# A hybrid encoder step: a third of the modulation's TensorE part goes to the vector engine, the rest is issued in bursts of four column groups

## The chip, the cores and the metric

The kernel runs on one core of a Trainium2 chip, as one program. The metric is the device time of one execution in microseconds (us); lower is better. The core has five engines that run side by side from queues of their own: PE (TensorE, matrix products), DVE (VectorE), ACT (ScalarE), POOL (GpSimd) and SP, which here only starts transfers from memory. Weight loads into the PE array are shown as an engine of their own, PEld.

## The reference, cut to what matters

One layer of a streaming encoder is computed for 256 prompt rows and 32 sample rows of width 2048. A vector `c` per sequence (two sequences, so two vectors) gives six modulation vectors of 2048 values:

```python
cs = jax.nn.silu(c)
mod = cs @ w_mod[l] + b_mod[l]                      # w_mod: 2048 x 12288, float32
sh1, sc1, g1, sh2, sc2, g2 = split(mod, 6)
h = rms_norm(x, norm1_g[l]) * (1 + sc1) + sh1
y, ... = mixer_block(h, ...)                        # w_in, three branches A, B, C, w_branch, w_out
x = x + g1 * y
h = rms_norm(x, norm2_g[l]) * (1 + sc2) + sh2
x = x + g2 * sq_relu_mlp(h, w_up[l], w_down[l])
y = rms_norm(x, final_g)
```

Part 0 and part 1 of the modulation (`sh1`, `sc1`) are needed before the first product, part 2 (`g1`, "the gate of the output projection") only when the output projection has been computed, and parts 3 to 5 later still.

## The kernel before, in words

All big products are float32 products made of three TensorE products each (high half times low half, high times high, low times high), on tiles of 128 x 128 weights against 288 or 290 columns. Weights arrive as 512 KB loads (`raw`, a ring of six buffers, started by SP in program order); ACT makes the high half `whi` (L425), DVE the low half `wlo` (L426), and PE takes both (L412 to L414 in the first stage, L443 to L445 after it). Every load of `w_mod` goes into the same ring of six.

The modulation has a batch of two, so its products are cheap to compute and dear to feed. It is a Python generator, `mods`, advanced one step (one load of 512 KB) at a time between the products. `mod_steps` makes a step; the rates `MODR`, `RS`, `RA`, `RB` ... say how many steps go with one piece of product work (1.5 in the first stage until parts 0 and 1 are through, then 0.2, and 0.4 from the first mixer of branch A).

- **The boot, parts 0 and 1** (`mod_stream`, L277): 8 units of 256 columns and 4 of 512. A load carries 4 row blocks of a 256 column unit or 2 of a 512 column unit. For each row block `k` the array's column group `k % 4` (32 of 128 columns, of which two are used) multiplies `cT` with the load; four groups work side by side and each sums its own quarter of the 16 row blocks. After a unit ACT copies the sums (L282), and `mod_flush` adds the four quarters with a product with `selm` (L348) and the bias on DVE (L349). A 256 column unit has 4 steps, a 512 column unit 8.
- **Part 2, the gate** (`mod_parts`, L329): two halves of 1024 columns, 16 loads each. Each load is one row block of 1024 columns, and four products of 256 columns, one in each column group, take it. After a half one copy and two transposes finish it.
- **Parts 4, 3 and 5** (`mod_part_ve`): four units of 512 columns, 8 loads of two row blocks each. DVE multiplies a load by the two scalars of each row block and adds, four instructions per load (L303 for the first two of a unit, L305 for all others), into two sums `macc`. At the end of a unit eight small products with `ones2` (L75 and L78), a copy and one transpose sum over the partitions.

A step is one load in each of the three forms, and each part has 32 steps, so the count of steps is the same in all. `together` (L72) issues the first of a list of instructions at ordinary priority and the rest right behind it. The order of the instructions on each engine is planned when the program is built, by a list scheduler with simulated times; `high_priority` moves the loads ahead.

One record of the trace is not one product: each float32 product of the modulation leaves two matmul records.

Of the kernel before, what the change touches and what calls it, by code (L numbers as in the profile page):

```python
# [10 lines left out]
F32 = mybir.dt.float32  # L11
# [3 lines left out]
ALU = mybir.AluOpType  # L15
PSUM = bass.MemoryType.PSUM

P = 128
D = 2048
NB = D // P  # L20
# [20 lines left out]
def tile_step(ctx, tc, io, outs):  # L41
    nc = tc.nc
    V, S, G, TE = nc.vector, nc.scalar, nc.gpsimd, nc.tensor

    const = ctx.enter_context(tc.tile_pool(name="const", bufs=1))
    wpool = ctx.enter_context(tc.tile_pool(name="wpool", bufs=3))
    hpool = ctx.enter_context(tc.tile_pool(name="hpool", bufs=3 * NB))
    pmain = ctx.enter_context(tc.tile_pool(name="pmain", bufs=4, space=PSUM))
    paux = ctx.enter_context(tc.tile_pool(name="paux", bufs=2, space=PSUM))

    PRIO = 2500

    MOD_PARTS = (2, 4, 3, 5)
    MOD_VE = (4, 3, 5)


    MODR, RS, RA, RB, RD, RW, RC = 1.5, 0.2, 0.4, 0.3, 0.5, 0.5, 0.25
# [2 lines left out]
    MTAG = ("raw", RAW)  # L60
# [8 lines left out]
    def nm(s):  # L69
        uid[0] += 1  # L70
        return f"{s}_{uid[0]}"

    def together(works):

        first = works[0]()  # L75
        with tc.issue_after(first.ins), tc.high_priority(offset=PRIO):
            for work in works[1:]:
                work()  # L78

    def aux():  # L80
        return paux.tile([P, 512], F32, tag="aux", name=nm("aux"))
# [28 lines left out]
    ident = const.tile([P, P], F32, name="ident")  # L110
# [62 lines left out]
    cT = const.tile([P, NB, 32], F32, name="cT")  # L173
    V.memset(cT, 0.0)
    with tc.high_priority(offset=2 * PRIO):
        ps = aux()
        TE.transpose(ps[:, 0:32], crow, ident[0:32, 0:32])
        S.activation(out=cT[:, :, 0:2].rearrange("p k s -> p s k"),
                     in_=ps[:, 0:32].rearrange("p (s k) -> p s k", s=2), func=AF.Silu)


    ones2 = const.tile([P, 2, 32], F32, name="ones2")
# [72 lines left out]
    def par(name, j, n=1):  # L255
        i, r = off[name]
        return pcols[i][:, r + j:r + j + n]
# [4 lines left out]
    mod = const.tile([P, 6 * NB, 2], F32, name="mod")  # L262
    wm = io["w_mod"][0].rearrange("(k p) n -> p k n", p=P)

    def mod_stream(units):

        for u, (c0, w) in enumerate(units):
            ps = paux.tile([P, 512], F32, tag="modps", name=nm("modps"), bufs=2)
            nk = 1024 // w
            for q in range(NB // nk):  # L270
                with tc.high_priority(offset=PRIO):
                    raw = wpool.tile([P, nk, w], F32, tag="raw", name=nm("raw"), bufs=RAW)
                    nc.sync.dma_start(out=raw, in_=wm[:, nk * q:nk * (q + 1), c0:c0 + w])
                for i in range(nk):
                    k = nk * q + i
                    cg = k % 4
                    TE.matmul(ps[32 * cg:32 * cg + 32, 0:w], cT[:, k, :], raw[:, i, :],  # L277
                              start=k < 4, stop=k >= 12)
                if q == NB // nk - 1:
                    with tc.high_priority(offset=PRIO):  # L280
                        sb = wpool.tile([P, 512], F32, tag="modsb", name=nm("modsb"), bufs=1)
                        S.copy(out=sb[:, 0:w], in_=ps[:, 0:w])  # L282
                    mod_tail.append((c0 // P, w // P, ps, sb))
                if q == 1:
                    mod_flush()
                yield
        mod_flush()

    def mod_part_ve(part):


        for u in range(4):
            c0 = part * D + u * 512
            acc = [wpool.tile([P, 512], F32, tag="macc", name=nm("macc"), bufs=2) for _ in range(2)]
            for q in range(8):
                with tc.high_priority(offset=PRIO):
                    raw = wpool.tile([P, 2, 512], F32, tag=MTAG[0], name=nm("mraw"), bufs=MTAG[1])
                    nc.sync.dma_start(out=raw, in_=wm[:, 2 * q:2 * q + 2, c0:c0 + 512])
                for i in range(2):
                    for s in range(2):  # L300
                        cs = cT[:, 2 * q + i, s:s + 1]
                        if q == 0 and i == 0:
                            V.tensor_scalar_mul(out=acc[s], in0=raw[:, i], scalar1=cs)  # L303
                        else:
                            V.scalar_tensor_tensor(out=acc[s], in0=raw[:, i], scalar=cs, in1=acc[s],  # L305
                                                   op0=ALU.mult, op1=ALU.add)
                if q == 1:
                    mod_flush()
                yield
            ps = paux.tile([P, 512], F32, tag="modps", name=nm("modps"), bufs=2)  # L310
            mod_tail.append((part * NB + u * 4, 0, ps, acc))
        mod_flush()

    def mod_parts(parts):


        for part in parts:
            if part in MOD_VE:
                yield from mod_part_ve(part)
                continue  # L320
            for half in range(2):
                ps = paux.tile([P, 512], F32, tag="modps", name=nm("modps"), bufs=2)
                c0 = part * D + half * 1024
                for k in range(NB):
                    with tc.high_priority(offset=PRIO):
                        raw = wpool.tile([P, 1024], F32, tag=MTAG[0], name=nm("mraw"), bufs=MTAG[1])
                        nc.sync.dma_start(out=raw, in_=wm[:, k, c0:c0 + 1024])
                    for cg in range(4):
                        TE.matmul(ps[32 * cg:32 * cg + 32, 0:256], cT[:, k, :], raw[:, cg * 256:(cg + 1) * 256],  # L329
                                  start=k == 0, stop=k == NB - 1)  # L330
                    if k == 1:
                        mod_flush()
                    yield
                with tc.high_priority(offset=PRIO):
                    sb = wpool.tile([P, 256], F32, tag="modsb", name=nm("modsb"), bufs=1)
                    S.copy(out=sb, in_=ps[:, 0:256])
                mod_tail.append((part * NB + half * 8, 0, ps, sb))
        mod_flush()

    mod_tail = []  # L340

    def mod_flush():

        while mod_tail:
            j, n, ps, sb = mod_tail.pop()
            if n:
                for b in range(n):
                    TE.matmul(ps[:, 2 * b:2 * b + 2], sb[:, b * P:(b + 1) * P], selm, start=True, stop=True)  # L348
                V.tensor_tensor(out=mod[:, j:j + n, :],  # L349
                                in0=ps[:, 0:2 * n].rearrange("p (b s) -> p b s", s=2),  # L350
                                in1=par("b_mod", j, n).unsqueeze(2).to_broadcast([P, n, 2]), op=ALU.add)
            else:
                nb = 2
                if type(sb) is list:
                    nb = 1
                    acc, sb = sb, wpool.tile([P, 256], F32, tag="modsb", name=nm("modsb"), bufs=1)
                    together([partial(TE.matmul, ps[32 * cg:32 * cg + 32, 0:P], ones2[:, s],
                                      acc[s][:, cg * P:(cg + 1) * P], start=s == 0, stop=s == 1)
                              for s in range(2) for cg in range(4)])
                    S.copy(out=sb[:, 0:P], in_=ps[:, 0:P])  # L360
                for b in range(nb):
                    TE.transpose(ps[:, b * P:(b + 1) * P], sb[:, b * P:(b + 1) * P], ident)
                v = ps[:, 0:nb * P].rearrange("p (b g r) -> p g b r", b=nb, r=32)
                m = mod[:, j:j + 4 * nb, :].rearrange("p (g b) s -> p g b s", b=nb)
                V.tensor_tensor(out=m, in0=v[:, :, :, 0:2], op=ALU.add,
                                in1=par("b_mod", j, 4 * nb).rearrange("p (g b) -> p g b", b=nb).unsqueeze(3)
                                .to_broadcast([P, 4, nb, 2]))


    KG = ((0, 2), (2, 2), (4, 2), (6, 2), (8, 4), (12, 4))  # L370
    boot = [(part * D + k0 * P, nk * P) for k0, nk in KG for part in (0, 1)]
    mods = chain(mod_stream(boot), mod_parts(MOD_PARTS))

    mod_count = [0]

# [82 lines left out]
    with tc.high_priority(offset=PRIO):  # L458
        for i in range(8):
            for c, src in ((c, xrow.get((c, i))) for c in range(3)):  # L460
                if src is not None:
                    n, w = src.shape
# [6 lines left out]
    ps = aux()  # L469
    for c, (t0, n) in enumerate(CH):  # L470
        TE.matmul(ps[:, t0:t0 + n], st[:, c, 8:9].to_broadcast([P, P]), ident if c < 2 else sel4,
                  start=True, stop=True)
# [569 lines left out]
    def finish_c(j, vt):  # L1042
        g = j // 2
        pm = aux()
        for c, (t0, n) in enumerate(CH):
# [11 lines left out]
    part = ([(COL_V, j, each(evac_v)) for j in range(0, 8, 2)] + [(COL_U, j, each(evac_u)) for j in range(0, 8, 2)]  # L1057
            + [(COL_XBC, j, each(evac_xbc)) for j in range(8, CVB, 2)]
            + [(COL_GATE + 2 * D, j, each(evac_gate0)) for j in range(0, G0, 2)])
# [7 lines left out]
    for g, (k0, nk) in enumerate(KG):  # L1067
# [7 lines left out]
        m = 4 // nk  # L1075
# [45 lines left out]
    ps = aux()  # L1121
# [36 lines left out]
    ps = transpose_xs()  # L1158
# [103 lines left out]
    parts = [0, NB - 2, NB - 1]  # L1262
# [10 lines left out]
    for q in range(4):  # L1273
        for c, (t0, n) in enumerate(CH):
            w = 2 * P if q == 3 else 4 * P
# [42 lines left out]
```

## Time and profile before

| | before |
|---|---|
| three timed runs | 2085.69, 2086.59, 2087.05 us; median 2086.59 |
| the profiled execution's own time | 2083.99 us |
| its span, first to last instruction | 2082.3 us (1.69 us lie around it) |
| granted TensorE clock, mean | 0.993 |
| PE, PEld, DVE, ACT, POOL busy | 98%, 93%, 70%, 48%, 7% of the span |
| read from memory | 405.05 MB, 197 GB/s over the span |

The profile is of one execution. Start times are counted from its first instruction. Matmuls are pipelined: the start of the next one, not the length of one, says what it took from the array. A busy time is a union of the instructions' spans, so overlaps are counted once.

### The profile page before, as it was taken

The numbers are of one execution on the slowest core, as the hardware profiler recorded it, in microseconds if no ns is written. First come the engines' busy times: TensorE is split into PE (matmuls) and PEld (weight loads), VectorE is DVE, ScalarE is ACT, GpSimd is POOL, SyncE is SP. The second block draws the span as 40 slices with busy tenths as digits, with TensorE's granted clock in tenths as the row PEclk, the third lists the DMA queues.
The fourth block names the chain that finished last, engine by engine and source line by source line (L and its number), as shares of the span: only waits on it lengthen the run. The fifth ranks groups of instructions, "written<-read, shape, count | busy, mean of one in ns | idle before, by whom it ended". The sixth has DMA issues, their size and how long they took to land.

```text
span 2082.3 us, 40240 instructions
## 1 busy us (share of the span) xinstructions
PE 2034.7 (98%) x16248; PEld 1941.9 (93%) x16248; DVE 1453.9 (70%) x2515; ACT 998.1 (48%) x1553; POOL 155.7 (7%) x284
## 2 busy tenths in 40 slices
PE   5999999999999999999999999999999999999997
PEld 3777898989999999999999999999999999999997
DVE  2566566776679987888889998665864455555564
ACT  3423475566555555645534455433443344334443
POOL 3020113011001110010100110000000000000010
PEclk8999999999999999999999999999999999999999
DMA  9888755455666665667777777666665555555552
GB/s 265 258 279 252 232 152 165 147 177 174 203 205 202 204 190 177 212 201 236 239 245 241 219 242 225 196 216 194 213 192 163 168 166 163 165 168 164 163 161 88
DMA packets 364874, 412.29 MB, mean 198 GB/s; under 512 B 14808, under 2 KB 325488, under 8 KB 364688
## 3 DMA queue, kind: packets, MB, share of 16 engines
q1 hardware_dynamic: 360784, 403.97, 62.6%
q0 software_dynamic: 3040, 4.58, 1.0%
q8 instruction: 127, 2.08, 0.4%
q10 hardware_dynamic: 864, 1.18, 0.2%
q14 instruction: 59, 0.48, 0.1%
HBM read 405.05 MB, written 4.62 MB: 197 GB/s over the span
## 4 chain that ended last, share of the span: by engine, by line
PE 60%; ACT 0%; DVE 0%; issue 0%; ACTq 0%
PE mm L445 20%; PE mm L443 20%; PE mm L444 20%; PE aux L1208 0%; PE aux L208 0%; ACT stage L1282 0%; PE aux L879 0%; PE modps L75 0%; PE modps L78 0%; PE aux L78 0%; PE aux L918 0%; PE aux L867 0%; PE aux L75 0%; PE aux L900 0%; PE pr L1265 0%; DVE x L1246 0%
## 5 line engine op out<-in xcount | busy, mean ns | idle before, releaser
L425 ACT CAST whi<-raw 128x1024 fp32r<-128x1024 f32 x568 | 595.2, 1048 | 862.3 <-PE mm L444 646.5
L426 DVE TENSOR_TENSOR wlo<-raw,whi 128x1024 fp32r<-128x1024 f32 x568 | 695.1, 1225 | 411.4 <-ACT whi L425 409.9
L443 PE MATMUL mm<-hlo,whi 128*128 128x288 f32 x1408 | 420.3, 299 | 0.0
L444 PE MATMUL mm<-hhi,whi 128*128 128x288 f32 x1408 | 417.0, 297 | 0.0
L445 PE MATMUL mm<-hhi,wlo 128*128 128x288 f32 x1408 | 414.0, 299 | 0.1
L444 PE MATMUL mm<-h2hi,whi 128*128 128x290 f32 x1024 | 303.5, 297 | 0.0
L445 PE MATMUL mm<-uhi,wlo 128*128 128x288 f32 x1024 | 303.2, 296 | 0.0
L443 PE MATMUL mm<-h2lo,whi 128*128 128x290 f32 x1024 | 303.0, 296 | 0.0
L445 PE MATMUL mm<-h2hi,wlo 128*128 128x290 f32 x1024 | 301.8, 297 | 0.0
L444 PE MATMUL mm<-uhi,whi 128*128 128x288 f32 x1024 | 301.3, 294 | 0.0
L443 PE MATMUL mm<-ulo,whi 128*128 128x288 f32 x1024 | 301.0, 294 | 0.0
L305 DVE SCALAR_TENSOR_TENSOR macc<-mraw,cT,macc 128x512 f32<-128x512 f32 x360 | 262.1, 755 | 26.1 <-DMA mraw<-in_w_mod_dram 25.7
L443 PEld LDWEIGHTS mm<-hlo,whi 128*128 128x128 f32 x1408 | 265.6, 189 | 9.1 <-issue 7.2
L444 PEld LDWEIGHTS mm<-hhi,whi 128*128 128x128 f32 x1408 | 266.0, 189 | 0.4
L445 PEld LDWEIGHTS mm<-hhi,wlo 128*128 128x128 f32 x1408 | 263.7, 189 | 1.7 <-DVE z L614 0.4
L443 PEld LDWEIGHTS mm<-h2lo,whi 128*128 128x128 f32 x1024 | 194.1, 190 | 0.5 <-DVE wlo L426 0.2
L445 PEld LDWEIGHTS mm<-h2hi,wlo 128*128 128x128 f32 x1024 | 193.6, 190 | 0.3 <-issue 0.2
L444 PEld LDWEIGHTS mm<-h2hi,whi 128*128 128x128 f32 x1024 | 193.8, 189 | 0.0
L443 PEld LDWEIGHTS mm<-ulo,whi 128*128 128x128 f32 x1024 | 193.0, 188 | 0.4 <-issue 0.4
L444 PEld LDWEIGHTS mm<-uhi,whi 128*128 128x128 f32 x1024 | 192.4, 188 | 0.0
L445 PEld LDWEIGHTS mm<-uhi,wlo 128*128 128x128 f32 x1024 | 192.2, 188 | 0.1
L412 PE MATMUL mm<-hlo,whi 128*128 128x288 f32 x448 | 139.1, 311 | 0.0
(420 smaller groups left out, 3068.9 us busy)
## 6 DMA issues: line engine op xcount, KB each, us to landing
raw<-in_w_in_dram SPq DMA_DIRECT2D x204, 512.0 KB, 4.3
mraw<-in_w_mod_dram SPq DMA_DIRECT2D x128, 512.0 KB, 4.1
raw<-in_w_up_dram SPq DMA_DIRECT2D x128, 512.0 KB, 3.7
raw<-in_w_down_dram SPq DMA_DIRECT2D x128, 512.0 KB, 3.5
raw<-in_w_mod_dram SPq DMA_DIRECT2D x64, 512.0 KB, 5.0
raw<-in_w_branch_dram SPq DMA_DIRECT2D x48, 512.0 KB, 4.3
raw<-in_w_out_dram SPq DMA_DIRECT2D x32, 512.0 KB, 4.6
raw<-in_w_in_dram SPq DMA_DIRECT2D x56, 256.0 KB, 5.0
```

The costliest lines, as they stand in the source:

```text
L305: V.scalar_tensor_tensor(out=acc[s], in0=raw[:, i], scalar=cs, in1=acc[s], op0=ALU.mult, op1=ALU.add)
L412: TE.matmul(pt, whi[:, i, cs], alo[k], start=i == 0, stop=False)
L425: S.copy(out=whi, in_=raw)
L426: V.tensor_sub(out=wlo, in0=raw, in1=whi)
L443: TE.matmul(pts[b], whi[:, i, cs], alo[k], start=k == 0, stop=False)
L444: TE.matmul(pts[b], whi[:, i, cs], ahi[k], start=False, stop=False)
L445: TE.matmul(pts[b], wlo[:, i, cs], ahi[k], start=False, stop=k == nk - 1)
```

## The change

Three things change, all in the modulation.

1. `mod_stream` collects the row blocks of two loads and issues them after every second load (`mod_cols`): eight products over four column groups for a 256 column unit, four products for a 512 column unit. They go through `together`, last row block first, so that the first one waits for the later load and the others follow it without other work between them.
2. Part 2 goes through `mod_part_ve` like the later parts; `mod_parts` and its branch in `mod_flush` are gone. Order and count of the steps stay: boot, then parts 2, 4, 3, 5, with 32 steps each.
3. The staging tile `modsb` of the tail is declared 128 wide in the room of 512.

```diff
-    MOD_VE = (4, 3, 5)
...
             nk = 1024 // w
+            held = []
             for q in range(NB // nk):
...
-                for i in range(nk):
-                    k = nk * q + i
-                    cg = k % 4
-                    TE.matmul(ps[32 * cg:32 * cg + 32, 0:w], cT[:, k, :], raw[:, i, :],
-                              start=k < 4, stop=k >= 12)
+                held += [(nk * q + i, raw[:, i, :]) for i in range(nk)]
+                if q % 2:
+                    mod_cols(ps, held, w)
+                    held = []
...
+    def mod_cols(ps, held, w):
+        works, begun = [], set()
+        for k, r in reversed(held):
+            cg = k % 4
+            works.append(partial(TE.matmul, ps[32 * cg:32 * cg + 32, 0:w], cT[:, k, :], r,
+                                 start=held[0][0] == 0 and cg not in begun, stop=k == held[0][0] + cg and held[-1][0] == NB - 1))
+            begun.add(cg)
+        together(works)
...
-    def mod_parts(parts):
-        for part in parts:
-            if part in MOD_VE:
-                yield from mod_part_ve(part)
-                continue
-            for half in range(2):
-                ps = paux.tile([P, 512], F32, tag="modps", name=nm("modps"), bufs=2)
-                c0 = part * D + half * 1024
-                for k in range(NB):
...
-                        raw = wpool.tile([P, 1024], F32, tag=MTAG[0], name=nm("mraw"), bufs=MTAG[1])
-                        nc.sync.dma_start(out=raw, in_=wm[:, k, c0:c0 + 1024])
-                    for cg in range(4):
-                        TE.matmul(ps[32 * cg:32 * cg + 32, 0:256], cT[:, k, :], raw[:, cg * 256:(cg + 1) * 256],
-                                  start=k == 0, stop=k == NB - 1)
...
-    mods = chain(mod_stream(boot), mod_parts(MOD_PARTS))
+    mods = chain(mod_stream(boot), *[mod_part_ve(part) for part in MOD_PARTS])
```

## Rows read from the trace of the kernel before

**Rows 1.** The page: busy time, share of the span, instructions.

```profile
PE 2034.7 (98%) x16248; PEld 1941.9 (93%) x16248; DVE 1453.9 (70%) x2515; ACT 998.1 (48%) x1553; POOL 155.7 (7%) x284
```

**Rows 2.** Windows: stretch, length, busy by engine (records), PE clock, DMA share, GB/s.

```profile
0.00:56.00 56.00, 30.96 (x221) 19.54 (x221) 12.06 (x32) 22.39 (x60) 17.82 (x52) 0.85 0.95 262
56.00:231.00 175.00, 175.00 (x1202) 131.02 (x1202) 103.86 (x211) 59.57 (x88) 11.18 (x21) 1.00 0.84 262
364.00:624.00 260.00, 254.32 (x2589) 235.34 (x2582) 185.62 (x446) 162.49 (x254) 24.24 (x60) 1.00 0.60 180
624.00:728.00 104.00, 102.53 (x989) 100.32 (x989) 97.03 (x200) 60.95 (x99) 12.59 (x27) 1.00 0.67 205
624.00:832.00 208.00, 204.44 (x1793) 200.78 (x1793) 180.84 (x347) 119.23 (x190) 21.81 (x49) 1.00 0.63 194
1144.00:1248.00 104.00, 104.00 (x808) 102.66 (x806) 102.36 (x189) 52.58 (x96) 15.58 (x12) 1.00 0.74 231
```

**Rows 3.** Timeline of PE in the boot: start, length, instruction, records merged.

```profile
59.82 0.29 PE L414 MATMUL mm<-hhi,wlo 128*128 128x288 f32 x1
60.05 0.64 PE L277 MATMUL modps<-raw,cT 128*32 128x256 f32 x8
60.62 0.40 PE L412 MATMUL mm<-hlo,whi 128*128 128x288 f32 x1
60.85 0.29 PE L413 MATMUL mm<-hhi,whi 128*128 128x288 f32 x1
60.98 0.29 PE L414 MATMUL mm<-hhi,wlo 128*128 128x288 f32 x1
...
70.61 1.06 PE L277 MATMUL modps<-raw,cT 128*32 128x256 f32 x14
...
121.66 1.04 PE L277 MATMUL modps<-raw,cT 128*32 128x512 f32 x2
...
127.20 1.07 PE L277 MATMUL modps<-raw,cT 128*32 128x512 f32 x8
128.20 0.40 PE L412 MATMUL mm<-hlo,whi 128*128 128x288 f32 x1
```

**Rows 4.** PE groups by shape, whole span, then from 56 to 231 us.

```profile
L277 PE MATMUL modps<-raw,cT 128*32 128x512 f32 x128 | 32.0, 604 | 0.0
L329 PE MATMUL modps<-mraw,cT 128*32 128x256 f32 x256 | 24.6, 391 | 1.3 <-DMA mraw<-in_w_mod_dram 1.3
...
L277 PE MATMUL modps<-raw,cT 128*32 128x256 f32 x144 | 16.6, 389 | 0.0
```

**Rows 5.** Windows of L329 alone: PE and PEld busy, clock, DMA share, GB/s.

```profile
364.00:624.00 260.00, 17.36 (x192) 4.24 (x184) 1.00 0.60 180
```

**Rows 6.** Timeline of PE around one tail of a DVE unit.

```profile
904.89 0.30 PE L445 MATMUL mm<-yhi,wlo 128*128 128x288 f32 x1
...
905.69 0.40 PE L443 MATMUL mm<-hlo,whi 128*128 128x288 f32 x1
```

**Rows 7.** DVE group of the sums: busy, mean ns, idle before.

```profile
L305 DVE SCALAR_TENSOR_TENSOR macc<-mraw,cT,macc 128x512 f32<-128x512 f32 x360 | 262.1, 755 | 26.1 <-DMA mraw<-in_w_mod_dram 25.7
```

**Rows 8.** Timeline of DVE where two sums follow each other.

```profile
644.61 1.41 DVE L305 SCALAR_TENSOR_TENSOR macc<-mraw,cT,macc 128x512 f32<-128x512 f32 x2
645.93 1.58 DVE L614 TENSOR_TENSOR z<-z,qA 128x144 f32<-128x144 f32 x7
```

**Rows 9.** Waits of SP's queue from 56 to 231 us: us, times, longest.

```profile
SPq L273 <- PE modps L277: 52.0, 25, 4.1
```

**Rows 10.** Windows of 13 us, as in rows 2.

```profile
156.00:169.00 13.00, 13.00 (x85) 8.99 (x84) 7.95 (x13) 3.75 (x4) 0.00 (x0) 1.00 0.98 317
```

**Rows 11.** Waits of PE, whole span: us, times, longest.

```profile
PE modps L277 <- DMA raw<-in_w_mod_dram: 14.6, 7, 6.8
```

**Rows 12.** Timeline of PE before the first product, at half clock.

```profile
16.34 1.08 PE L277 MATMUL modps<-raw,cT 128*32 128x256 f32 x8 [0.46 <-DMA raw<-in_w_mod_dram]
17.98 1.08 PE L277 MATMUL modps<-raw,cT 128*32 128x256 f32 x8 [0.56 <-DMA raw<-in_w_mod_dram]
```

More of the change, by code (lines that the diff above doesn't have):

```diff
@@ L312, in mod_part_ve @@
         mod_flush()
-    def mod_parts(parts):
-        for part in parts:
-            if part in MOD_VE:
-                yield from mod_part_ve(part)
-                continue
-            for half in range(2):
-                ps = paux.tile([P, 512], F32, tag="modps", name=nm("modps"), bufs=2)
-                c0 = part * D + half * 1024
-                for k in range(NB):
-                    with tc.high_priority(offset=PRIO):
-                        raw = wpool.tile([P, 1024], F32, tag=MTAG[0], name=nm("mraw"), bufs=MTAG[1])
-                        nc.sync.dma_start(out=raw, in_=wm[:, k, c0:c0 + 1024])
-                    for cg in range(4):
-                        TE.matmul(ps[32 * cg:32 * cg + 32, 0:256], cT[:, k, :], raw[:, cg * 256:(cg + 1) * 256],
-                                  start=k == 0, stop=k == NB - 1)
[L331 to L338, printed above, removed]
     mod_tail = []
@@ L352, in mod_flush @@
             else:
[L353 to L367, printed above, removed]
+                sums, sb = sb, wpool.tile([P, P], F32, tag="modsb", name=nm("modsb"), bufs=1, padded_shape=[P, 512])
+                together([partial(TE.matmul, ps[32 * cg:32 * cg + 32, 0:P], ones2[:, s],
+                                  sums[s][:, cg * P:(cg + 1) * P], start=s == 0, stop=s == 1)
+                          for s in range(2) for cg in range(4)])
+                S.copy(out=sb, in_=ps[:, 0:P])
+                TE.transpose(ps[:, 0:P], sb, ident)
+                V.tensor_tensor(out=mod[:, j:j + 4, :], in0=ps[:, 0:P].rearrange("p (g r) -> p g r", r=32)[:, :, 0:2],
+                                in1=par("b_mod", j, 4).unsqueeze(2).to_broadcast([P, 4, 2]), op=ALU.add)
     KG = ((0, 2), (2, 2), (4, 2), (6, 2), (8, 4), (12, 4))
     boot = [(part * D + k0 * P, nk * P) for k0, nk in KG for part in (0, 1)]
-    mods = chain(mod_stream(boot), mod_parts(MOD_PARTS))
+    mods = chain(mod_stream(boot), *[mod_part_ve(part) for part in MOD_PARTS])
     mod_count = [0]
```

## The prediction

> **What bounds the kernel now.** I read the page first, then the busy times of stretches, then the timeline of PE around the modulation's products, and last the waits. The page says that PE is busy for 98% of the span [rows 1]. The windows tell where that is more than a modelled overlap: from 56 to 231 us PE has no idle time at 175.00 of 175.00 us, while the DMA engines are busy 0.84 of it; from 364 to 624 us, the mixers of branch A, PE is busy 254.32 of 260.00 us and DVE 185.62; later stretches look alike [rows 2]. Only the first 56 us are not PE's: it is busy 30.96 of them, DMA 0.95 [rows 2], and PE waits there for loads of the modulation, 14.6 us in 7 waits [rows 11]. So an instruction taken off PE after 56 us is worth its time in PE's stream, unless the next resource stands close behind: DMA in the boot, DVE in the mixers.
>
> **What a burst costs PE.** The big products start every 0.13 us (60.85 to 60.98). A burst of four 256 column products, one in each column group (8 records), comes between the product at 59.82 and the one at 60.62; the one after starts at 60.85. That is 1.03 us for two intervals that otherwise take 0.26: a burst costs 0.77 us. A burst of four 512 column products is busy for 1.07 us and a burst of a single one for 1.04 [rows 3]: one product alone costs what four in four groups cost. Start to next start at 127.20 is 1.00 us, the same distance as 59.82 shows ahead of it (0.23) and the slower next product (0.10) added and one interval taken off, so 1.2 us per burst. Seven 256 column products in one run are busy 1.06 us (70.61) [rows 3]: eight, two in each group, cost 1.2 us too.
>
> **Part 2 leaves PE.** Its products are busy 24.6 us [rows 4], which at 0.64 each is 38 bursts (32 if none had been split up); 38 x 0.77 = 29.3 us. Bounds: 24.6 if nothing but their own time came back, 29.3. I take 29.3, since the slow handover is in the rows at every burst. What comes in: four tails of eight small products. One stands between 904.89 and 905.69 [rows 6]: 0.80 less 0.13, and 0.10 for the slow next one, 0.77 us; four make 3.1. The transposes stay four. ACT gets four copies for two, hidden, since it is half idle [rows 1]. Net -26.2 us on PE.
>
> **Part 2 goes to DVE.** 32 loads x 4 instructions. L305 is busy 262.1 us for 360, 0.73 us each [rows 7], 2.9 us a load. In the mixers' stretch stand 192 of the 256 records of part 2 [rows 5], 24 loads: 24 x 2.9 = 69.9 us. DVE's 185.62 there [rows 2] becomes 255.5. PE's share of the same stretch falls from 260 by 17.36 / 0.64 = 27 bursts x 0.77 = 20.9 and rises by three tails, 2.3: 241.4. So by busy time DVE would need 14 us more than PE leaves. But DVE's busy time shrinks where instructions follow closely: two sums and the start of what follows lie 1.32 us apart (644.61 to 645.93), 0.66 each against a mean length of 0.755 [rows 7, 8]; 24 loads are then 63.4 us. If half of the 446 instructions already there [rows 2] save the same 0.09 us when packed, 20 us more go: 229 us, 0.95 of 241.4. A DVE at 0.98 with PE idle for nothing is shown: 102.36 of 104.00 us from 1144 to 1248, though without mixers; with mixers, 97.03 of 104.00 [rows 2]. Bounds in this stretch: 0, if packing does it all, and 14, if it does nothing; below nothing is excluded, since no work leaves DVE. I take the middle, +7 us. What queues behind the sums on DVE is `wlo` and the mixers' short steps, and PE waits for both. The loads lose nothing: DMA is at 0.60 there [rows 2].
>
> The Trainium skill, Perfetto Trace Analysis, section Identifying the Most-Contended Engine, calls occupancy a fair measure of an engine's limit for Vector; by that rule DVE sets this stretch at 255.5 us, the term is +14 and the sum 7 us later than mine. The same page, section Optimizing Scalar/DVE Operations, says that about half of an instruction's fixed overhead overlaps with the next one; the rows at 644.61 agree with that (0.66 against 0.755), which is why I do not follow occupancy to the end.
>
> **The boot in pairs.** After 56 us: the 512 column products are busy 32.0 us [rows 4], at 1.05 each 30 bursts; they become 16 (4 units x 16 products in fours), 14 x 1.2 = 17 us less. The 256 column products there are busy 16.6 us for 144 records [rows 4]; 72 products become 9 bursts of eight, 9 x 1.2 = 10.8, against 16.6 and about 22 handovers of 0.13, 19.5: 9 us less. PE's floor falls by 26, from 175 to 149 us. The loads: 175 us at 262 GB/s and a share of 0.84 [rows 2]; the fullest 13 us show 0.98 and 317 GB/s [rows 10], at which the same bytes take 145 us at best. Both floors lie together, and the ring of six lies between them: SP waits 52.0 us (25 times) and 18.3 us (9 times) for a buffer that the modulation's products hold [rows 9]. A pair now holds the first buffer until the second load has landed, about 2.0 us longer (512 KB at 262 GB/s). Bounds: -26 if PE's time all comes back, +5 if the held buffers starve the products (PE's 26 us of room used up, and a quarter of the 25 waits longer by one landing, some 13 us less the 8 that a stream half as bursty gives back). I take -10, nearer to the floor of loads than to PE's.
>
> The Trainium skill, DMA: Bandwidth & Descriptors, section Bandwidth, gives about 358 GB/s as one core's limit to memory; by that the boot's bytes take 128 us, loads would not bind, and the term is PE's -26. No run here shows more than 317 GB/s over 13 us.
>
> **The first 56 us.** Bursts here wait for loads. Two bursts 1.64 us apart become one that starts with the second load; at half clock four products take 1.08 us [rows 12], eight some 1.9, so a unit ends about 0.8 us later, and the first buffer of a pair comes free one landing later. Bounds 0 to +4 (five pairs before the first product); I take +1.
>
> **The sum.** -29.3 + 3.1 + 7 - 10 + 1 = -28.2 us. The profiled execution's own time is 2083.99; 2055.8 by it. The median of the runs shown is 2.6 higher, 2086.59, and 28.2 less is 2058.4. I predict 2058 us.
>
> **The rivals.**
> - *Everything comes back.* DVE packs and loads keep up: -29.3 + 3.1 - 26 + 0 = -52, 2034 us. For it: 102.36 of 104.00 on DVE with PE full; against it: the ring's waits [rows 2, 9]. 0.10.
> - *The pairs starve the boot*, while the gate's part works: -29.3 + 3.1 + 7 + 5 + 2 = -12, 2074 us. For it: 25 waits on exactly these buffers [rows 9]; against it: every burst frees two at once. 0.12.
> - *DVE becomes the bound of the mixers and hands the gain back.* With mixers the highest share shown is 97.03 / 104.00 = 0.933 [rows 2]. If that is a ceiling of busy time, the stretch takes 255.5 / 0.933 = 273.9 us, 32.5 over PE's 241.4, in place of +7: -2.7, 2084 us, hardly a change. This is what the skill's occupancy rule, named above, comes to with a ceiling below one. 0.11.
> - *The same ceiling lower, and the kernel is slower.* Over 624 to 832 us DVE stands at 180.84 / 208 = 0.87 [rows 2] with the same sums in the mixers. If chains through DVE cannot be served above that, 255.5 / 0.87 = 293.7, +52 in place of +7: +17, 2104 us. The sum turns positive at a stretch of 276.6 us, a ceiling of 0.924. Against it: PE was not waiting for DVE in those 208 us, so 0.87 was what was asked for, not what was possible. 0.09.
>
> **How the numbers follow.** My forecast has 0.58 (2044 to 2072 as its own range: DVE 0 to +14, boot -18 to 0). Faster by over 0.2% (4 us, about what a measurement of this kernel can tell): the forecast, the first two rivals and a part of the third, 0.58 + 0.10 + 0.12 + 0.04 = 0.84; within 0.2%: the rest of the third, 0.07; slower: 0.09. The range from 2040 to 2080 leaves out most of the first rival, the third and the fourth, together about 0.2.
>
> **What would show it.** Right: no L329; L277 in bursts of 16 records (256 columns) and 8 (512), some 26 us less of PE from 56 us to the boot's end, of which about 10 show in where the boot ends; L305 at 480 records, half as many again over the mixers' stretch; PE's time from there to the end of branch A shorter by some 12 to 20 us; all behind the mixers unchanged. Wrong: in the windows, PE with idle time in the mixers and waits of PE on DVE or of `whi` and `wlo` behind the sums, or SP waiting longer for L277 than now with DMA below 0.84 in the boot. The plan of the instructions is made anew for the whole program, and an unlucky order in the mixers would be such a wait at a place that no row shows.

## The result and the profile after

| | before | after |
|---|---|---|
| median, us (4 runs each) | 2086.14 (2085.23 to 2087.05) | 2064.70 (2063.41 to 2066.30) |
| ratio, 95% interval | | 0.9898 (0.988 to 0.9915) |
| profiled execution: own time, span, us | 2083.99, 2082.3 | 2066.30, 2064.6 |

The change takes 21.4 us, 1.0%. The forecast was 28.2. The profiled execution of after is the longest of its four, so the two traces lie 17.7 us apart.

Code after the changed functions has moved up by 23 lines: L412 to L414 are now L389 to L391, L443 to L445 are L420 to L422, `whi` and `wlo` are made at L402 and L403, and the sums of L305 stand at L315. L277 has become `together`'s two lines, L74 (first of a burst) and L77 (the others).

The page of after: the busy line that answers to [rows 1], then groups (line, engine, operation, tiles, count, busy time, mean ns, idle before them).

```profile
PE 1994.1 (97%) x16056; PEld 1939.7 (94%) x16056; DVE 1532.2 (74%) x2645; ACT 1001.9 (49%) x1558; POOL 154.4 (7%) x284
...
L420 PE MATMUL mm<-hlo,whi 128*128 128x288 f32 x1408 | 420.2, 300 | 12.8 <-ACT whi L402 7.8
...
L422 PE MATMUL mm<-hhi,wlo 128*128 128x288 f32 x1408 | 410.0, 299 | 6.4 <-DVE wlo L403 6.3
L315 DVE SCALAR_TENSOR_TENSOR macc<-mraw,cT,macc 128x512 f32<-128x512 f32 x480 | 349.3, 755 | 19.4 <-DMA mraw<-in_w_mod_dram 18.3
```

PE has lost 40.6 us of busy time, twice what the kernel got faster: PE is idle where it was not, and its share fell from 98% to 97%. The last column of the two big products says where. L315 has its 480 records, at the mean of [rows 7].

Windows of after (columns as in [rows 2]); the last four are the places with the lower clock from 220 to 620 us.

```profile
0.00:56.00 56.00, 25.18 (x196) 18.12 (x200) 11.25 (x32) 20.79 (x56) 17.71 (x52) 0.88 0.92 249
56.00:220.00 164.00, 161.99 (x1286) 138.17 (x1287) 115.16 (x234) 63.73 (x98) 10.85 (x21) 1.00 0.94 299
220.00:340.00 120.00, 112.49 (x836) 108.15 (x835) 97.20 (x160) 82.67 (x137) 25.09 (x32) 0.97 0.54 160
340.00:600.00 260.00, 242.14 (x2420) 234.44 (x2419) 233.60 (x522) 159.25 (x247) 22.38 (x57) 0.98 0.60 179
1120.00:1224.00 104.00, 104.00 (x807) 102.56 (x807) 101.48 (x183) 50.63 (x91) 16.85 (x12) 1.00 0.74 231
286.20:293.00 6.80, 4.76 (x18) 4.47 (x19) 4.16 (x6) 6.74 (x11) 0.00 (x0) 0.50 0.26 77
351.00:354.40 3.40, 3.40 (x16) 3.40 (x17) 3.40 (x11) 0.86 (x2) 0.00 (x0) 0.51 0.04 12
508.10:511.50 3.40, 3.40 (x16) 3.40 (x15) 3.21 (x9) 1.82 (x3) 0.00 (x0) 0.50 0.13 46
579.70:583.10 3.40, 3.40 (x16) 3.40 (x15) 1.70 (x5) 2.42 (x5) 0.00 (x0) 0.51 0.51 154
```

Two stages moved in opposite ways. The boot moves its bytes at 299 GB/s and a DMA share of 0.94, where it moved 262 at 0.84 [rows 2]. In the mixers of branch A (340 to 600 us, the same stage as 364 to 624 before) PE is busy 242.14 of 260 us and idle 17.9, where it was idle 5.7; DVE is up from 185.62 to 233.60. Four stretches stand at the lower level of TensorE's clock, 1.2 GHz (granted clock 0.50 and 0.51). PE worked 4.76 + 3 x 3.40 = 15.0 us in them. Two big products in the first of them (start, length, instruction):

```profile
290.39 0.44 PE L422 MATMUL mm<-hhi,wlo 128*128 128x288 f32 x1
290.63 0.44 PE L420 MATMUL mm<-hlo,whi 128*128 128x288 f32 x1
```

They start 0.24 us apart, where 0.13 is the distance at the upper level [rows 3]; so the 15.0 us cost some 7 more than they would there, an estimate. Behind the mixers nothing changed: 104.00 of 104.00 on PE, and the stage stands some 18 us earlier.

Waits of PE in after, 200 to 620 us (us, times, longest). Before, none of these three stood there for a microsecond.

```profile
PE mm L420 <- ACT whi L402: 7.4, 4, 4.9
PE mm L422 <- DVE wlo L403: 6.3, 6, 2.7
PE mm L420 <- ACT iv L563: 3.7, 1, 3.7
```

PE waits for the two halves into which each weight block is split, and for the mixers' own steps on ACT. Two of these waits, by timelines of after (start, length, instruction, records merged, in brackets the idle time before): first PE and DVE at the longest wait for `wlo`, then ACT and DVE at the longest for `whi`.

```profile
400.08 0.30 PE L420 MATMUL mm<-hlo,whi 128*128 128x288 f32 x1
400.22 0.29 PE L421 MATMUL mm<-hhi,whi 128*128 128x288 f32 x1
403.16 0.40 PE L422 MATMUL mm<-hhi,wlo 128*128 128x288 f32 x1 [2.65 <-DVE wlo L403]
```

```profile
398.85 1.94 DVE L686 RECIPROCAL rms<-rms 128x288 f32<-128x288 f32 x1
400.71 0.24 DVE L587 TENSOR_TENSOR z<-bA 128x144 f32<-128x144 f32 x1
...
401.69 0.28 DVE L588 TENSOR_TENSOR z<-bA 128x128 f32<-128x128 f32 x1
401.89 1.22 DVE L403 TENSOR_TENSOR wlo<-raw,whi 128x1024 fp32r<-128x1024 f32 x1
```

```profile
283.77 1.28 ACT L772 ACT_TABLE_LOAD   x1
285.06 0.44 ACT L772 ACTIVATE ldt<-ldt 16x288 f32<-16x288 f32 x1
285.52 1.28 ACT L773 ACT_TABLE_LOAD   x1
286.82 0.44 ACT L773 ACTIVATE ldt<-ldt 16x288 f32<-16x288 f32 x1
287.17 1.03 ACT L402 CAST whi<-raw 128x1024 fp32r<-128x1024 f32 x1
```

```profile
282.10 0.75 DVE L315 SCALAR_TENSOR_TENSOR macc<-mraw,cT,macc 128x512 f32<-128x512 f32 x1
287.29 0.45 DVE L774 SCALAR_TENSOR_TENSOR dt<-zdt,ldt 16x288 f32<-16x288 f32 x1 [4.45 <-ACT ldt L773]
```

At 400 us DVE works without a gap, and `wlo` is made behind a reciprocal and the mixer's steps on `z`; no sum stands right before it. That sums further ahead (four, from 391.85 us) have put the queue back is argued, not shown. At 287 us it is not DVE, which is itself idle for 4.45 us: the `whi` that PE needs stands on ACT behind activations that load a table each. Of all waits in that view some 13 us end on ACT and some 11 on DVE, so a late DVE is at most a part of the story.

Waits of SP's queue in after, 56 to 220 us, answering to [rows 9]; then PE's wait for loads over the whole span, answering to [rows 11].

```profile
SPq L274 <- PE modps L77: 26.4, 15, 4.1
SPq L382 <- PE modps L77: 17.2, 8, 4.3
```

```profile
PE modps L74 <- DMA raw<-in_w_mod_dram: 21.1, 5, 11.1
```

The modulation's own loads (L274) wait half as long for buffers that its products hold (52.0 to 26.4 us, 25 to 15 times), and the longest wait is still 4.1; the weights' loads (L382) wait for them as before (18.3 us then). PE waits 21.1 us for the modulation's loads, 6.5 more than before, all but 1.5 of it in the first 56 us.

Timeline of PE in after around a burst of eight 256 column products (16 records).

```profile
82.79 0.29 PE L391 MATMUL mm<-hhi,wlo 128*128 128x288 f32 x1
83.01 0.40 PE L74 MATMUL modps<-raw,cT 128*32 128x256 f32 x1
83.02 0.42 PE L77 MATMUL modps<-raw,cT 128*32 128x256 f32 x3
83.25 0.38 PE L74 MATMUL modps<-raw,cT 128*32 128x256 f32 x1
83.26 0.82 PE L77 MATMUL modps<-raw,cT 128*32 128x256 f32 x11
84.01 0.40 PE L389 MATMUL mm<-hlo,whi 128*128 128x288 f32 x1
84.25 0.30 PE L390 MATMUL mm<-hhi,whi 128*128 128x288 f32 x1
```

From 82.79 to 84.25 are 1.46 us for two intervals of 0.13: the burst costs 1.20 us, the value of the working.

The groups of the boot's last product row in after (duration in ns, first and last start in us).

```profile
L389 PE MATMUL mm<-hlo,whi x448: 289/295/609, 44.4 to 276.3; 128*128 128x288 f32 x150
```

Before, this group ran from 41.8 to 291.8: the first big product starts 2.6 us later, the last 15.5 earlier. What stands ahead of the last one differs. 42 of the mixer's 48 products for dt, some 5.6 us, came behind it before; and five bursts of the gate (40 records), some 3.9 us, stood ahead of it before and are gone. With both counted, the boot's work ends some 17 us earlier, and from its first to its last product it takes some 20 us less.

### The profile page after: what moved, and what is told of

The parts are those of the page before. It is cut to its first block, busy times and chain, and to the rows that moved or that the text cites. A ratio compares the mean times of both kernels' runs of the same rounds, so it can differ in the third digit from the quotient of the medians.

```text
span 2064.6 us, 40004 instructions
## 1 busy us (share of the span) xinstructions
PE 1994.1 (97%) x16056; PEld 1939.7 (94%) x16056; DVE 1532.2 (74%) x2645; ACT 1001.9 (49%) x1558; POOL 154.4 (7%) x284
## 4 chain that ended last, share of the span: by engine, by line
PE 77%; ACT 2%; DVE 1%; issue 0%; ACTq 0%; DVEq 0%
PE mm L422 24%; PE mm L420 24%; PE mm L421 24%; PE aux L77 1%; ACT whi L402 0%; DVE wlo L403 0%; PE aux L856 0%; PE modps L74 0%; PE aux L657 0%; PE aux L1185 0%; PE modps L77 0%; PE aux L74 0%; PE aux L668 0%; ACT L589 0%; PE aux L555 0%
## 5 line engine op out<-in xcount | busy, mean ns | idle before, releaser
L402 ACT CAST whi<-raw 128x1024 fp32r<-128x1024 f32 x568 | 595.3, 1049 | 836.0 <-PE mm L421 626.1
L403 DVE TENSOR_TENSOR wlo<-raw,whi 128x1024 fp32r<-128x1024 f32 x568 | 696.1, 1227 | 372.7 <-ACT whi L402 370.8
L420 PE MATMUL mm<-hlo,whi 128*128 128x288 f32 x1408 | 420.2, 300 | 12.8 <-ACT whi L402 7.8
L422 PE MATMUL mm<-hhi,wlo 128*128 128x288 f32 x1408 | 410.0, 299 | 6.4 <-DVE wlo L403 6.3
L315 DVE SCALAR_TENSOR_TENSOR macc<-mraw,cT,macc 128x512 f32<-128x512 f32 x480 | 349.3, 755 | 19.4 <-DMA mraw<-in_w_mod_dram 18.3
L420 PE MATMUL mm<-h2lo,whi 128*128 128x290 f32 x1024 | 304.4, 298 | 0.0
L422 PE MATMUL mm<-uhi,wlo 128*128 128x288 f32 x1024 | 303.2, 296 | 0.0
L422 PE MATMUL mm<-h2hi,wlo 128*128 128x290 f32 x1024 | 301.8, 297 | 0.0
L420 PE MATMUL mm<-ulo,whi 128*128 128x288 f32 x1024 | 301.0, 294 | 0.0
L420 PEld LDWEIGHTS mm<-hlo,whi 128*128 128x128 f32 x1408 | 266.7, 189 | 15.6 <-ACT whi L402 9.5
L422 PEld LDWEIGHTS mm<-hhi,wlo 128*128 128x128 f32 x1408 | 262.7, 189 | 9.7 <-DVE wlo L403 8.5
L422 PEld LDWEIGHTS mm<-h2hi,wlo 128*128 128x128 f32 x1024 | 194.3, 191 | 0.3 <-issue 0.2
L420 PEld LDWEIGHTS mm<-h2lo,whi 128*128 128x128 f32 x1024 | 193.6, 189 | 0.5 <-issue 0.4
L420 PEld LDWEIGHTS mm<-ulo,whi 128*128 128x128 f32 x1024 | 193.0, 188 | 0.4 <-issue 0.4
L422 PEld LDWEIGHTS mm<-uhi,wlo 128*128 128x128 f32 x1024 | 192.2, 188 | 0.1
L389 PE MATMUL mm<-hlo,whi 128*128 128x288 f32 x448 | 137.0, 306 | 1.8 <-DVE hlo L489 1.4
```

What stands on the lines that cost most here:

```text
L389: TE.matmul(pt, whi[:, i, cs], alo[k], start=i == 0, stop=False)
L402: S.copy(out=whi, in_=raw)
L403: V.tensor_sub(out=wlo, in0=raw, in1=whi)
L420: TE.matmul(pts[b], whi[:, i, cs], alo[k], start=k == 0, stop=False)
L422: TE.matmul(pts[b], wlo[:, i, cs], ahi[k], start=False, stop=k == nk - 1)
```

## The experiments

Each was compared with the kernel before on the same chip (three chips, medians of before 2086.88, 2086.15 and 2085.12). Intervals are of the ratio.

| kernel | gate on TensorE / DVE, units | median, us | ratio |
|---|---|---|---|
| boot in pairs alone | as before / 0 | 2064.72 | 0.9898 (0.9878 to 0.9918) |
| gate on DVE alone, boot as before | 0 / 4 | 2076.24 | 0.9955 (0.9942 to 0.9969) |
| gate as units of 512 in pairs | 4 / 0 | 2061.63 | 0.9889 (0.9870 to 0.9908) |
| 60 of the gate's 128 sums left out | 0 / 4 | 2047.67 | 0.9820 (0.9805 to 0.9836) |
| half of the units | 2 / 2 | 2051.98 | 0.9834 (0.9819 to 0.9849) |
| pairs for 512 columns only | as before / 0 | 2064.52 | 0.9897 (0.9881 to 0.9914) |
| four loads at a time | as before / 0 | 2083.14 | 0.9984 (0.9972 to 0.9997) |
| other rates of the steps | 0 / 4 | 2063.22 | 0.9889 (0.9874 to 0.9904) |
| three units on TensorE | 3 / 1 | 2066.40 | 0.9909 (0.9893 to 0.9926) |
| one unit on TensorE | 1 / 3 | 2058.75 | 0.9874 (0.9859 to 0.9889) |
| 88 of the gate's 128 sums left out | 0 / 4 | 2049.95 | 0.9823 (0.9807 to 0.9838) |
| half of the units, pairs for 512 only | 2 / 2 | 2052.74 | 0.9842 (0.9828 to 0.9857) |

### Either part alone

The first is the kernel before with the new `mod_stream` and `mod_cols` only:

```diff
+    MOD_VE = (4, 3, 5)
-    mods = chain(mod_stream(boot), *[mod_part_ve(part) for part in MOD_PARTS])
+    mods = chain(mod_stream(boot), mod_parts(MOD_PARTS))
```

> The boot in pairs alone, the gate on TensorE as in the kernel before. Theory A (the pairs are worth some 19 us and the gate's move nothing, because the mixers give its 26 us back in idle time and lower clock): 2067 us, within 3 of the changed kernel. Rival B (the gate's move is worth 10 us or more and the pairs the rest): 2075 us or more. Rival C (the mixers lose because everything in them is planned anew and comes earlier, not because of the sums on DVE): the loss shows here too, 2080 us, with over 15 us of PE idle in the mixers.

The second is the kernel before with the gate's part on DVE:

```diff
-    MOD_VE = (4, 3, 5)
+    MOD_VE = (2, 4, 3, 5)
```

> The gate's move to DVE alone, the boot as before. Theory A: 2083 to 2088 us, no change that counts, with L329's 24.6 us gone and PE idle in the mixers up from 8 us to some 20. Rival B: 2070 to 2076. Rival C: 2064 to 2070, since the boot ends where it did and the mixers are not shifted.

The pairs alone give 2064.72, the time of the whole change (2064.70). The gate's move alone gives some 10 us, at the edge of what Rival B expected; behind the pairs it gives nothing. So the parts do not add up, and most of the gain is not the gate's, as the working had it.

Windows of the pairs alone, the mixers; then the stretch from 240 to 620 us of the gate alone, and of after. Columns as in [rows 2].

```profile
340.00:600.00 260.00, 254.79 (x2595) 235.16 (x2596) 183.94 (x446) 159.30 (x248) 25.54 (x63) 1.00 0.60 180
...
240.00:620.00 380.00, 372.45 (x3486) 347.59 (x3479) 270.59 (x598) 243.70 (x395) 48.15 (x93) 1.00 0.59 176
```

```profile
240.00:620.00 380.00, 364.52 (x3322) 353.62 (x3321) 335.49 (x685) 238.51 (x384) 46.12 (x88) 0.96 0.58 175
```

```profile
240.00:620.00 380.00, 355.93 (x3281) 345.49 (x3280) 335.33 (x696) 246.97 (x393) 48.29 (x96) 0.98 0.58 174
```

With the gate on TensorE, PE is idle for 380 - 372.45 = 7.6 us of this stretch, at a mean granted clock of 1.00. With it on DVE, 15.5 us and a granted clock of 0.96 in the old boot, 24.1 us and 0.98 in after. The profiled execution of the gate alone took 2081.29 us, the longest of its seven; the median is 5 us lower, so its 0.96 may overstate what the clock takes there.

### The gate in pairs on TensorE

```diff
-    mods = chain(mod_stream(boot), *[mod_part_ve(part) for part in MOD_PARTS])
+    gate = [(2 * D + u * 512, 512) for u in range(4)]
+    mods = chain(mod_stream(boot + gate), *[mod_part_ve(part) for part in MOD_PARTS[1:]])
```

> Boot in pairs, and the gate on TensorE too, as four more 512 column units in pairs of loads: 16 bursts of 1.2 us (19 us) where the kernel before has 38 of 0.77 (29 us). Theory A: the mixers keep DVE as free as before, so 10 us less than with the gate in single loads: 2055 to 2058 us, faster than the changed kernel. Rival D (the mixers are bound by their own chains whatever PE is relieved of): 2064 to 2068.

2061.63: the gate on TensorE in the new bursts is at least as fast as on DVE, but only some 3 us were saved against the pairs alone, of the 10 expected. A burst of eight 512 column records that stands alone costs 1.19 us by the starts around it (at 238.67, 300.37, 388.33 us and others), the 1.2 of the working. By the same reading the 16 bursts with their tails take some 22 us of PE's stream, where 36 of the old ones take some 27: the expectation left the tails out. And PE is idle for 9.9 us from 240 to 620 us (7.6 in the pairs alone).

### DVE relieved, PE as after

`s` is the sequence whose sum is formed; the kernel leaves out the gate's sums of the second sequence but for the first of each unit, so 60 of 128 instructions of part 2 are gone (L315 has 420 records for 480), and PE's work is that of after.

```diff
-                        else:
+                        elif part != 2 or s == 0:
```

> The changed kernel with half of the gate's sums left out: the second sequence's sums of part 2 stop after the first row block, so its gate is not what the reference has; loads, PE's work and the order of the steps stay. Theory A (DVE's load in the mixers is what gives the 26 us back): 45 us less of DVE, PE idle in the mixers down from 24 us to about 12, 2050 to 2056 us. Rival C (the new order does it) : 2062 to 2066.

Next, 88 of the 128 are left out (the "three quarters" of the expectation):

```diff
-                        else:
+                        elif part != 2 or (s == 0 and i == 1):
```

> The changed kernel with three quarters of the gate's sums left out: of part 2 only every second row block is summed and only for the first sequence, so the gate is not what the reference has; PE's work, the loads and the order of the steps stay. Theory A: 71 us less of DVE than in the changed kernel, all of PE's 22 us come back: 2042 to 2046, below the half sums (2047.7). Rival F (something other than DVE's fill, as the held buffers of the ring, takes the rest): 2046 to 2050, no gain over the half sums.

Windows of the first of the two, the mixers and the longer stretch.

```profile
340.00:600.00 260.00, 254.81 (x2551) 248.38 (x2550) 221.06 (x508) 157.64 (x253) 24.96 (x63) 0.99 0.61 187
...
240.00:620.00 380.00, 368.42 (x3448) 359.03 (x3447) 314.08 (x673) 241.17 (x394) 44.15 (x90) 0.98 0.59 178
```

With PE's work unchanged, leaving out 60 sums brings PE back from 242.14 to 254.81 us in the mixers, and the kernel from 2064.70 to 2047.67, 17 us. From 240 to 620 us PE's idle time falls from 24.1 to 11.6 us, near the 7.6 of the pairs alone, while the mean granted clock stays at 0.98; the other 4 us or so lie elsewhere (the first big product starts at 42.5 us, 1.9 earlier). This is the test of the cause: with half of the sums most of the idle time goes. The waits for `whi` go with it, though they end on ACT; whether the sums made ACT late or only changed the planned order is not told apart. Leaving out more of them gives nothing further (2049.95, PE idle for 12.9 us), where Theory A expected 2042 to 2046; it is what Rival F expected. Buffers held by the sums, Rival F's example, do not stand out: SP's queue waits 25.0 us for them from 220 to 620 us in after, less than the 67.0 us for the gate's products on TensorE before (240 to 640 us).

### Two units here, two there

```diff
-    def mod_part_ve(part):
+    def mod_part_ve(part, units=range(4)):
...
-        for u in range(4):
+        for u in units:
...
+    gate = [(2 * D + u * 512, 512) for u in (0, 1)]
+    mods = chain(mod_stream(boot + gate), mod_part_ve(2, (2, 3)), *[mod_part_ve(part) for part in MOD_PARTS[1:]])
```

> Boot in pairs; of the gate's four units of 512 columns two go on TensorE in pairs and two on DVE. Theory A (DVE's load in the mixers gives PE's gain back, the more the fuller DVE is): two units on PE cost some 11 us of the 22, DVE gets 47 us of sums for 94 and gives back about 5: 2055 to 2060 us, faster than the changed kernel and than the pairs alone. Rival D (nothing comes back from the mixers whatever one does there): 2062 to 2068.

```profile
340.00:600.00 260.00, 253.05 (x2538) 243.85 (x2538) 231.32 (x527) 163.17 (x257) 24.09 (x60) 0.99 0.62 188
```

That row is the mixers' window of this kernel. 2051.98 us: it computes everything, and beats both kernels, by 34 us (1.7%) and by 12.7. DVE is as busy here as in after (231.32 against 233.60), yet PE has 253.05 us: the busy share of DVE alone does not decide.

The other divisions change the `(0, 1)` and `(2, 3)` above to `(0, 1, 2)` and `(3,)`, and to `(0,)` and `(1, 2, 3)`:

> Boot in pairs; three of the gate's four units on TensorE in pairs, one on DVE (24 us of sums). Theory A, with what the half units showed (47 us of sums give back little): PE saves some 9 us against the pairs alone, DVE gives back 1 or 2: 2055 to 2058, between the half units (2052) and the pairs alone (2064.7). Rival E (the half units were fast by a lucky order and not by the dose): anywhere, 2048 to 2066, with no order in the dose.

> Boot in pairs; one unit of the gate on TensorE in pairs, three on DVE (71 us of sums). Theory A: PE saves some 17 us against the pairs alone, DVE gives back about 10: 2056 to 2061, between the half units and the changed kernel (2064.7). Rival E: no order in the dose.

The kernel with one unit on TensorE came as expected, 2058.75. The one with three came at 2066.40, where Theory A expected 2055 to 2058. Its waits of PE, 240 to 620 us:

```profile
PE aux L74 <- ACT vA L558: 3.1, 1, 3.1
PE aux L556 <- DVE atc L618: 3.0, 1, 3.0
PE modps L342 <- ACT modsb L341: 3.0, 1, 3.0
PE aux L556 <- ACT iv L564: 2.9, 2, 2.2
```

These are single waits inside the mixers' chains and one in a tail of the modulation; `wlo` takes only 1.1 us. Every variant's instructions are planned anew over the whole program, and Rival E, that the order and not the dose decides, is not excluded. PE's idle time from 240 to 620 us, by the number of the gate's units on DVE and with the boot in pairs:

| units on DVE | 0 | 1 | 2 | 3 | 4 |
|---|---|---|---|---|---|
| PE idle, us | 7.6 (9.9 with the gate in pairs) | 16.8 | 11.2 | 17.4 | 24.1 |

All four on DVE have the most and none the least, but one unit, with the fewest sums, has more than two: an order alone can be worth some 6 us of idle time. Why in this one stays open.

### How the boot's gain is made

Pairs for the units of 512 columns only; the 256 column units issue after every load, but through `together`:

```diff
-                if q % 2:
+                if q % 2 or w == 256:
```

> The gate on TensorE as before; only the four 512 column units of the boot go in pairs, the eight of 256 columns stay at single loads, though each load's four products are now issued together. If the burst's fixed price is the cause, the 512 column units carry about 17 of the 26 us of PE time: 2068 to 2072 us. If it is that products of one burst are no longer torn apart by others, the 256 column units give their part too without pairs: 2064 to 2067.

2064.52, as with all in pairs (2064.72). Pairing the 256 column units is worth nothing that can be told here once each load's four products go through `together`, as the second expectation had it; before, other products tore many of them apart, and a single one costs 0.74 us of the stream (63.19 and 66.46 us in the trace of before) where four in four groups cost 0.77. For 512 columns a load alone holds two products, and pairing them fills the four groups. `together` without pairs for these was not run. SP's queue waits 56.0 us here (27.6 and 28.4) for buffers that the products hold, 43.6 in after (26.4 and 17.2): the gain does not hang on these waits. The same edit to the kernel with two units here and two there:

> The half units, with pairs only for the units of 512 columns (the boot's eight units of 256 columns load by load, each load's products together). By what pairs of 512 alone showed, the pairs of 256 columns are worth nothing: 2049 to 2054, the same as the half units.

2052.74 against 2051.98: the same answer, and the fastest kernel's time a second time, on another chip.

Four loads at a time, in the kernel with the boot in pairs alone:

```diff
-                if q % 2:
+                if q % 4 == 3:
```

> The gate on TensorE as before; the boot's loads are collected four at a time. Bursts fall from 32 to 16 (some 4 us less on PE), but four of the six buffers are held at once. If the ring binds the boot: longer waits for loads in the boot, 2070 us or more. If the loads still keep ahead, as with pairs: 2060 to 2064.

```profile
56.00:224.00 168.00, 155.22 (x1243) 132.28 (x1243) 99.20 (x211) 60.39 (x95) 10.34 (x21) 1.00 0.87 282
```

That row is the window of its boot. Fewer bursts, but PE is idle for 12.8 us where after is idle for 2.0, and the loads fall back from 299 to 282 GB/s: 2083.14, nearly all of the gain gone. (The profiled execution is the fastest of its ten, 2076.86.) Four of the six buffers of the ring are held. In this window PE waits 3.9 us for the modulation's loads (1.5 in after), 6.6 for `acc`, the running sums of the big products, and 1.6 for `whi`; so the slower loads that the second rival feared are there, one step further than the change went, though most of PE's waits do not end on them. How `acc` comes late stays open.

### Other rates of the steps

In after, the steps of the modulation are drawn less often in branch A's mixers and more often in B's:

```diff
-    MODR, RS, RA, RB, RD, RW, RC = 1.5, 0.2, 0.4, 0.3, 0.5, 0.5, 0.25
+    MODR, RS, RA, RB, RD, RW, RC = 1.5, 0.2, 0.25, 0.4, 0.5, 0.5, 0.25
```

> The changed kernel with the modulation's steps moved from branch A's mixers to branch B's: rate 0.25 for 0.4 in A, 0.4 for 0.3 in B; the work is the same. Theory A: PE's idle time falls in the mixers of A (24 us there now, to some 14) and DVE, fuller in B, gives back less there than it gains here: 2056 to 2062. Rival C (idle time from the new order, not from DVE's fill): 2063 to 2068.

2063.22, hardly below after's spread: a microsecond above what Theory A expected, and just within Rival C's range. PE is idle for 16.6 us from 240 to 620 us, 7.5 less than in after; from 600 to 660 us it is idle for 4.2 at a mean granted clock of 0.93, some 8 us in all, with waits for `whi` (2.6 us) and `wlo` (2.5) (after: 1.3 us idle, 1.00). So what A's mixers gained was lost again in B's; that the sums cost the same wherever they are put is not shown by one such shift.

## Why the prediction was right, and where its terms were not

The time (2064.7, forecast 2058, within 2040 to 2080) and the direction came out, in part by luck. What leaves PE and what comes in were right, and the two large terms were wrong in opposite directions, the boot by 10 us and DVE by 15: -27.7 + 3.1 + 22 - 20 is some -23, near the -21.4 measured. (The chances outside the range add up to nearly 0.3 in the working, with most of the first rival, and not to 0.2.)

- **What a burst costs: right.** 1.20 us for eight 256 column products. The records of the modulation's tiles on PE fell as counted: in the mixers from 21.75 us of busy time (the pairs alone) to 3.66. By the timeline 36 bursts stand in the mixers there; at 0.77 they are 27.7 us, and four new tails at 3.1 leave 24.6, near the forecast 26.2.
- **The boot, -10: mis-sized.** The last product of the boot is 18.5 us earlier in the pairs alone (273.3), where the order is the old one, and some 17 in after; from the first product (44.1 and 44.4) to the last the stage got shorter by some 20 us, most of the way to PE's floor of -26. The step that failed is "nearer to the floor of loads than to PE's". By its own rows the floor of loads, 145 us, lies below PE's 149 and allows the whole -26; -10 is only the middle of its two bounds. It took the fullest 13 us (317 GB/s, [rows 10]) as out of reach for the whole boot, and the ring's waits [rows 9] as lost transfers. After shows 299 GB/s and 0.94 over 164 us, and 319 GB/s over the 52 us from 69 to 121, so 317 was no rate of 13 us alone; the ring's waits changed little for the weights' loads, and the boot got its time all the same. The Trainium skill, DMA: Bandwidth & Descriptors, section Bandwidth, has some 358 GB/s for one core; its result, a boot bound by PE alone, was nearer than mine, although no run here went above 301 GB/s over such a stretch (the kernel with 88 sums left out).
- **The first 56 us, +1: not told apart.** The first big product starts 2.6 us later in after, but as late (44.4) in the gate alone, which has no pairs, and at 41.5 with two units here and two there, which has them. PE's longest wait for a load is 11.1 us (6.8 before, [rows 11]). The "half clock" of [rows 12] was read off the lengths, 1.08 us for 0.64; the windows there show a granted clock of 1.00.
- **DVE in the mixers, +7: the step that failed.** It measured about 22. Against the pairs alone, PE is idle 16.5 us longer from 240 to 620 us (372.45 less after's 355.93 of busy time, by the windows of that stretch), and the lower clock costs some 5 us more (7, less some 2 that the pairs alone lose in one such stretch at 316 us). Together some 22, against 24.6 that PE was spared: the move is worth next to nothing, and after and the pairs alone stand at the same median. The step took the middle between 0 and 14, both bounds from busy time: whether DVE has room on average. But PE waits for one instruction at a time: 2.65 us at 400 for a `wlo` whose queue had no gap, 4.9 at 288 for a `whi` on ACT, which is half idle, while DVE is idle too. No bound from busy time holds that. How much of the 22 is the sums' weight and how much the new order is open.
- **The third rival, at 0.11, had the outcome in the mixers, not the mechanism.** The gate's gain was handed back; its 2084 kept the boot at -10 and took 32.5 for the mixers, and each missed by some 10. Its ceiling of busy time does not hold: two units here and two there have DVE at 231.32 of 260 and PE at 253.05, after has it at 233.60 and PE at 242.14. The Trainium skill, Perfetto Trace Analysis, section Identifying the Most-Contended Engine, by which DVE's occupancy sets the limit, gave +14. It pointed the right way, and fell short of the 22: DVE stood at 233.60 of 260 us, not full, while PE waited.
- **The clock** was in no term. PE ran at the upper level through A's mixers before (1.00, [rows 2]). In after each stretch at the lower level stands at a place where PE had just been idle, the longest (286.2 to 293.0) at the wait of 4.9 us for `whi`; but not every wait is followed by one, and behind the 2.65 us at 400 the granted clock stays at 1.00.
- **The second rival** (held buffers starve the boot) did not come with pairs, and in part with four loads; the first (2034) fell with the mixers.

What stays open: why the gate's move gains 10 us in the old boot and nothing in the new one, and why three units on TensorE are slow. Each variant has another order of instructions throughout, so differences of some 5 us between them cannot be put down to one edit.

## What to carry to other kernels

Count the bursts in which small products break into a dense stream, not the products: four in four column groups cost PE about what one costs (0.77 and 0.74 us for 256 columns), so collect just enough to fill the groups, and no more loads than the ring can spare. Before work goes to an engine at 70%, ask what a busy engine waits for from it: the room there is in time between two such due results, not in the busy share; and try half of the work too: here it was the fastest of the five divisions, though the times are not in the order of the share. A total that comes out near the forecast proves none of its terms: only each part by itself showed that the boot's gave all.

## What the runs showed of the hardware

- One core's loads of the modulation and of weights moved 299 GB/s over 164 us at a DMA share of 0.94 while PE was busy 161.99 us of it, and 319 GB/s over 52 us of that (69 to 121) at a share of 1.00.
- Short idle stretches of PE can cost more than themselves: in after, waits of 1.2 to 4.9 us stand at or just before the start of four stretches of 3.4 to 6.8 us at the lower level of the clock, some 7 us in all beside 24 us of idle time from 240 to 620 us. A wait of 2.65 us was followed by none.
- A burst of column-tiled products in a dense stream costs about the same for one as for four groups: 0.74 and 0.77 us for 256 columns, 1.17 and 1.19 for 512 (121.66 and 127.20 us in before), and 1.20 for eight products of 256.
